# SSD stage of a hybrid encoder: masked product on VectorE, y gathered two chunks behind, decays times C made in place

## The chip, the cores and the metric

One core of a Trainium2 chip runs the whole program. The metric is the device time of one execution in microseconds (us), as the median of several. Engines: PE multiplies matrices, DVE is VectorE, ACT is ScalarE, POOL is GpSimd, SP is SyncE, which here issues DMAs.

## The reference, cut to what matters

Two layers on 1024 tokens of width 1024 in f32: dilated attention, then a bidirectional Mamba-2 SSD. The change concerns the second. For one direction, with 32 heads in 8 groups of 4, a state of 128 and chunks of 128 tokens:

```python
xbc = silu(depthwise_conv5(h @ w_in) + conv_b)
xdt = x * dt
acs = cumsum(dt * a)                           # within a chunk
decay = exp(where(lower, acs[l] - acs[s], -inf))
cb = einsum('bclgn,bcsgn->bcgls', C, B)
y_diag = einsum('bcgrls,bcsgrp->bclgrp', cb * decay, xdt)
states = einsum('bclgn,bclgrp->bcgrpn', B, xdt * exp(acs[-1] - acs))
prev = scan(states, exp(acs[-1]))              # state before each chunk
y_off = einsum('bclgn,cbgrpn->bclgrp', C, prev) * exp(acs)
```

The two directions and a skip term x d are added, the sum is multiplied by silu(z), normalised and projected back.

## The kernel before

**What runs beside what.** Layer 1 goes through the 8 groups. `group_dense(g)` makes the projection of group g: six tiles (x0, x1, B, C, z0, z1) of 128 channels x 1024 tokens, each in eight steps of six matmuls (L352 to L354; the f32 weights are split into a high part on ACT, L253, and a low part on DVE, L254). The first four tiles go through the convolution: ACT takes the middle tap out of PSUM (L1298), and four pairs of operations on DVE (L1306) add the other taps, straight from the accumulators. `ssd_items(g)` lists the SSD work of group g with weights, and `weave` puts it, in proportion to the weights, between the steps of the end of group g and the beginning of group g+1; for the last group it is woven into the output projection (`out1`: L976 to L978, with its y preparation L1485, L1502, L1507, L1508). What is emitted in this order is the order of every engine's queue.

**Accumulators.** Two of four PSUM banks hold a tile. Its four tap pairs are emitted in the tile that follows, behind steps 0, 1, 3 and 5, and the tile after that writes the same banks.

**The chunks of a group.** Behind the transposes (`A1`, L1364) and states (`A2`, L1376, L1377) come the chunks c from 7 down to 0, with four pieces:

- `B0(c)`: a DMA of 512 KB on SP (L1391) loads the decays, spread over all partitions, into `acs`, a pool of two buffers.
- `B1(c)`: ACT makes `ea`, the exponential of `acs` (L1401), DVE makes the four exponents E (L1404), PE the product of C and B (L1407), DVE masks it into cb (L1410), ACT takes the exponential of E (L1412) and writes four copies W of cb times dt (L1414). Then the load for c-2 is issued.
- `M(c)`: DVE multiplies ea by C in place (L1423), adds the other direction's cb times dt to W (L1428), and E times W, the masked product, is made on POOL, or on DVE in the last group and in chunk 0 (L1430).
- `B2(c)`: PE gathers y (L1441; 24 matmuls, 16 in chunks 7 and 0) from the states with ea and from x with the product; DVE adds the skip term (L1445, a pair of operations), POOL multiplies by silu(z) (L1449, two operations), and the last chunk sends the group's y to DRAM (L1454).

Before, `B2(c+1)` stands between `B1(c)` and `M(c)`. `dirs(c)` leaves out the direction that has no state yet, so the decays of chunks 7 and 0 have half the width.

Of the kernel before, what the change touches and what calls it, by code (L numbers as in the profile page):

```python
# [17 lines left out]
P = 128  # L18
# [55 lines left out]
class Trunk:  # L74
# [1272 lines left out]
    def ssd_items(self, g):  # L1347
# [7 lines left out]
        def ck(c):  # L1355
            return slice(P * c, P * c + P)
# [30 lines left out]
                    nc.vector.tensor_add(s, p, w)  # L1387

        def B0(c):
            a = live["a", c] = self.u("acs", [P, 2, 4, P], F32, 2)  # L1390
            nc.sync.dma_start(a, self.acsd[c, :, hs][None].to_broadcast([P, 2, 4, P]))  # L1391

        def dirs(c):
# [1 line left out]
            return [d for d, k in ((0, c > 0), (1, c < C - 1)) if k]  # L1395

        def B1(c):
            a = live.pop(("a", c))
            ea = live["ea", c] = self.u("ea", [P, 2, 4, P], F32, 2)
            ds = slice(dirs(c)[0], dirs(c)[-1] + 1)  # L1400
            nc.scalar.activation(ea[:, ds], a[:, ds], AF.Exp)  # L1401
            E, W = live["G", c] = [self.u("G", [P, 4, P], F32, 5) for _ in range(2)]
            for h in range(4):
                nc.vector.scalar_tensor_tensor(E[:, h], a[:, 0, h], self.delta[:, c, 4 * g + h:4 * g + h + 1], a[:, 1, h],  # L1404
                                               op0=OP.add, op1=OP.min)
            p = self.bank("a0", [P, P], 2)
            nc.tensor.matmul(p, st["B"][:, ck(c)], st["C"][:, ck(c)], start=True, stop=True)  # L1407
            cb = live["cb", c] = self.u("cb", [P, 2, P])
            tri = self.cst[:, CST["upper"][0]:CST["lower"][1]].rearrange("p (d l) -> p d l", d=2)
            nc.vector.tensor_mul(cb, p[:, None].to_broadcast([P, 2, P]), tri)  # L1410
            for h in range(4):
                nc.scalar.activation(E[:, h], E[:, h], AF.Exp, bias=self.nacb[:, c, 4 * g + h:4 * g + h + 1])  # L1412
            for h in range(4):
                nc.scalar.activation(W[:, h], cb[:, 0], AF.Copy, scale=self.dt[:, c, 4 * g + h:4 * g + h + 1])  # L1414
            if c == 0 and g < 7:
                nc.scalar.preload_act_table_set(SILU)
            if c > 1:
                B0(c - 2)

        def M(c):  # L1420
            ds = dirs(c)
            ea = live["ea", c][:, ds[0]:ds[-1] + 1].rearrange("p d h l -> p (d h) l")
            nc.vector.tensor_mul(ea, ea, st["C"][:, None, ck(c)].to_broadcast([P, 4 * len(ds), P]))  # L1423
            cb = live.pop(("cb", c))
            E, W = live["G", c]
            for h in range(4):
                hh = 32 + 4 * g + h
                nc.vector.scalar_tensor_tensor(W[:, h], cb[:, 1], self.dt[:, c, hh:hh + 1], W[:, h],  # L1428
                                               op0=OP.mult, op1=OP.add)
            (nc.vector if g == 7 or c == 0 else nc.gpsimd).tensor_mul(E, E, W)  # L1430

        def B2(c):

            y = self.bank("a3" if c % 2 else "a2", [P, 2, P])
            G, _ = live.pop(("G", c))
            ea = live.pop(("ea", c))
            for r in range(2):
                mms = [(SS[6 - c if d else c - 1][:, d], ea[:, d]) for d in dirs(c)] + [(xt[c], G)]
                for k, (w, m) in enumerate(mms):
# [17 lines left out]
        for j in range(C // 2):  # L1457
            items += [(200, lambda c=c: A1(c)) for c in (j, C - 1 - j)]
            if j:
                items.append((900, lambda j=j: A2(j - 1)))  # L1460
        items.append((1, lambda: (B0(C - 1), B0(C - 2))))
        items += [(900, lambda j=j: A2(j)) for j in range(C // 2 - 1, C)]
        if g == 7:
            items.append((1500, lambda: None))
        for c in range(C - 1, -1, -1):
            items.append((900, lambda c=c: B1(c)))
            if c < C - 1:
                items.append((500, lambda c=c: B2(c + 1)))
            items.append((1150, lambda c=c: M(c)))
        items += [(800, lambda: None), (500, lambda: B2(0))]  # L1470
        return items

    def out1(self, tail):
# [269 lines left out]
```

## Time and profile before

| | us |
|---|---|
| median of 3 runs (lowest, highest) | 1907.08 (1903.09, 1907.57) |
| the profiled execution | 1906.58 |
| its span in the profile | 1904.7 |

| engine | busy us | share of the span |
|---|---|---|
| PE | 1792.7 | 94% |
| DVE | 1404.3 | 74% |
| ACT | 957.8 | 50% |
| POOL | 392.7 | 21% |

The granted clock of PE was 0.98 of full speed over the span. A share is a mean over stages with different limits. A row of a timeline below gives start, duration, engine, line and operation, result and operands with their shapes, how many instructions are grouped (x4), and in brackets the idle time before it with what ended it. Group 2 of the SSD stage, which lies at 1207 to 1301 us, stands for the six groups 1 to 6, which have one pattern.

### The profile page before, as it was taken

To read this page: it belongs to the slowest core of one execution; us is meant where nothing else is said; L and a number is where in the kernel's file an instruction comes from. 1 tells how busy PE (TensorE), PEld (TensorE's weight loads), DVE (VectorE), ACT (ScalarE), POOL (GpSimd) and SP (SyncE) were. 2 spreads that over 40 slices of the span, in tenths; PEclk is the share of its full clock that TensorE was granted. 3 is DMA by queue.
4 is the path that set the end of the run, shared out by engine and by line. 5 is a ranking of instruction groups with operands and counts; after the bars stand their busy time and mean duration, and the time that the engine had idled before them with its cause. 6 is when DMAs were issued, how large, how long until landed. Compare 5 with 4: busy or idle time off the path is not lost.

```text
span 1904.7 us, 28678 instructions
## 1 busy us (share of the span) xinstructions
PE 1792.7 (94%) x10050; PEld 1450.5 (76%) x10050; DVE 1404.3 (74%) x3171; ACT 957.8 (50%) x2089; POOL 392.7 (21%) x541
## 2 busy tenths in 40 slices
PE   5899999999999999999989999999999999888997
PEld 3678788777788887779767777777777777666787
DVE  7867568667664665566767888888888888888875
ACT  5454445444454555444434655555555656555632
POOL 4611122112211311000101211212121212323310
PEclk7899999999999999999989999999999999999999
DMA  6242234222311321355113333333333333344643
GB/s 255 86 130 81 81 107 134 84 87 83 105 53 54 80 60 49 93 185 175 56 49 80 104 85 94 84 94 84 94 84 94 86 92 90 110 123 123 204 152 103
DMA packets 99735, 193.67 MB, mean 102 GB/s; under 512 B 15624, under 2 KB 23048, under 8 KB 99592
## 3 DMA queue, kind: packets, MB, share of 16 engines
q1 hardware_dynamic: 86600, 167.32, 28.9%
q0 software_dynamic: 12288, 23.86, 4.6%
q8 instruction: 80, 1.31, 0.3%
q10 hardware_dynamic: 704, 0.66, 0.1%
q14 instruction: 63, 0.52, 0.1%
HBM read 169.00 MB, written 16.48 MB: 97 GB/s over the span
## 4 chain that ended last, share of the span: by engine, by line
PE 26%; DVE 21%; ACT 6%; issue 3%; DMA 2%; POOL 0%; DVEq 0%; SPq 0%; ACTq 0%; POOLq 0%
DVE big L1306 5%; PE acc L352 4%; DVE G L1404 4%; PE acc L354 4%; PE acc L353 4%; DVE G L1428 3%; DVE ea L1423 3%; PE a L1377 3%; DVE wlo L254 2%; PE a L978 2%; PE a L976 2%; PE a L977 2%; PE acc L978 1%; PE acc L977 1%; PE acc L976 1%
## 5 line engine op out<-in xcount | busy, mean ns | idle before, releaser
L352 PE MATMUL acc<-big,whi 128*128 128x512 f32 (+1 forms) x1520 | 637.7, 420 | 24.0 <-ACT big L275 12.5
L353 PE MATMUL acc<-big,whi 128*128 128x512 f32 (+1 forms) x1520 | 596.9, 393 | 3.2 <-DVE big L276 3.1
L354 PE MATMUL acc<-big,wlo 128*128 128x512 f32 (+1 forms) x1520 | 597.1, 393 | 0.3 <-DVE wlo L254 0.3
L352 PEld LDWEIGHTS acc<-big,whi 128*128 128x128 f32 x1520 | 288.5, 190 | 88.3 <-issue 28.4
L354 PEld LDWEIGHTS acc<-big,wlo 128*128 128x128 f32 x1520 | 288.0, 189 | 65.1 <-DVE wlo L254 1.2
L353 PEld LDWEIGHTS acc<-big,whi 128*128 128x128 f32 x1520 | 289.5, 190 | 51.7 <-DVE big L276 6.5
L254 DVE TENSOR_TENSOR wlo<-wraw,whi 128x512 fp32r<-128x512 f32 (+1 forms) x298 | 214.4, 724 | 132.7 <-ACT whi L253 129.3
L253 ACT CAST whi<-wraw 128x512 fp32r<-128x512 f32 (+1 forms) x302 | 182.1, 611 | 84.5 <-PE a L977 27.4
L671 ACT ACTIVATE sm<-sm,nb 128x256 f32<-128x256 f32 (+1 forms) x192 | 89.3, 466 | 198.4 <-DVE nb L669 195.9
L1306 DVE SCALAR_TENSOR_TENSOR big<-acc,cv,big 128x512 f32<-128x512 f32 (+1 forms) x248 | 173.0, 740 | 2.2 <-ACT big L1298 2.2
L1412 ACT ACTIVATE G<-G,nacb 128x128 f32<-128x128 f32 x256 | 84.3, 391 | 154.9 <-DVE G L1404 154.1
L1430 POOL TENSOR_TENSOR G<-G,G 128x512 f32<-128x512 f32 x49 | 68.8, 1405 | 392.5 <-DVE G L1428 327.7
L682 DVE COPY pt<-a 128x512 f32<-128x512 f32 (+1 forms) x96 | 57.6, 600 | 76.5 <-PE a L680 76.5
L666 DVE CUSTOM_DVE_ANT_0 sm<-a,cst 128x256 f32<-128x256 f32 (+1 forms) x192 | 65.0, 376 | 64.3 <-PE a L661 64.0
L568 POOL DMA_DIRECT2D rt<-kT x92 | 50.5, 563 | 248.9 <-ACT kT L508 150.5
L1404 DVE SCALAR_TENSOR_TENSOR G<-acs,delta 128x128 f32<-128x128 f32 x256 | 99.3, 448 | 0.0
L976 PE MATMUL a<-big,whi 128*128 128x256 f32 (+1 forms) x304 | 99.3, 327 | 0.0
L978 PE MATMUL a<-big,wlo 128*128 128x256 f32 (+1 forms) x304 | 98.1, 323 | 0.9 <-DVE wlo L254 0.9
L977 PE MATMUL a<-big,whi 128*128 128x256 f32 (+1 forms) x304 | 97.9, 322 | 0.0
L1449 POOL TENSOR_TENSOR big<-big,yt 128x128 f32<-128x128 f32 x128 | 63.3, 515 | 159.5 <-DVE yt L1445 159.5
L976 PE MATMUL acc<-big,whi 128*128 128x512 f32 x224 | 91.1, 407 | 1.2 <-ACT big L253 1.2
L977 PE MATMUL acc<-big,whi 128*128 128x512 f32 x224 | 88.9, 397 | 2.4 <-DVE big L254 2.4
(255 smaller groups left out, 3198.5 us busy)
## 6 DMA issues: line engine op xcount, KB each, us to landing
wraw<-in_win SPq DMA_DIRECT2D x186, 256.0 KB
acs<-acsd SPq DMA_DIRECT2D x64, 512.0 KB
wraw<-in_wout SPq DMA_DIRECT2D x112, 256.0 KB
big<-in_modw SPq DMA_DIRECT2D x48, 512.0 KB
yd<-big POOLq DMA_DIRECT2D x14, 512.0 KB, 4.9
big<-yd SPq DMA_DIRECT2D x28, 256.0 KB
vT<-mix POOLq DMA_DIRECT2D x20, 256.0 KB, 4.5
big<-in_xT SPq DMA_DIRECT2D x8, 512.0 KB
```

The source lines that it names most:

```text
L253: self.nc.scalar.copy(dst_hi, src)
L254: self.late.append((lambda: self.lo_engine.tensor_sub(dst_lo, src, dst_hi.bitcast(F32)), tile))
L352: mm(o, hi[:, cols], x_[:, t0:t0 + n], start=first, stop=False, **kw)
L353: mm(o, hi[:, cols], x_[:, H2 + t0:H2 + t0 + n], start=False, stop=False, **kw)
L354: mm(o, lo[:, cols], x_[:, t0:t0 + n], start=False, stop=last, **kw)
L671: nc.scalar.activation(sm[:, h, :W], sm[:, h, :W], AF.Exp, bias=nb[:, h:h + 1], scale=0.125, accum_out=stat[:, h, 1, i:i + 1])
L976: mm(o, hi[:, c], x[:, t:t + n], start=kt == 0 and (n == H2 or m % 2 == 0), stop=False, **kw)
L977: mm(o, hi[:, c], x[:, H2 + t:H2 + t + n], start=False, stop=False, **kw)
L978: mm(o, lo[:, c], x[:, t:t + n], start=False, stop=kt == nkt - 1, **kw)
L1306: nc.vector.scalar_tensor_tensor(y[:, lo:hi], a[:, lo + o:hi + o], w[:, cv, k:k + 1], y[:, lo:hi], op0=OP.mult, op1=OP.add)
L1404: nc.vector.scalar_tensor_tensor(E[:, h], a[:, 0, h], self.delta[:, c, 4 * g + h:4 * g + h + 1], a[:, 1, h], op0=OP.add, op1=OP.min)
L1412: nc.scalar.activation(E[:, h], E[:, h], AF.Exp, bias=self.nacb[:, c, 4 * g + h:4 * g + h + 1])
```

## The change

- The masked product runs on DVE in all groups and chunks, behind the W add and ahead of decays times C.
- `acs` gets four buffers, and the exponential and decays times C are made in place in them; the pool `ea` goes. ACT makes that exponential behind the W copies instead of first. E and W get pools of three and two in place of five shared buffers.
- `B2(c+2)` stands between `B1(c)` and `M(c)`; `B2(1)` and `B2(0)` come at the end.
- The load `B0(c-1)` is issued ahead of `M(c)`, one at a time, in place of that for c-2 at the end of `B1(c)`.

```diff
         def B0(c):
-            a = live["a", c] = self.u("acs", [P, 2, 4, P], F32, 2)
+            a = live["a", c] = self.u("acs", [P, 2, 4, P], F32, 4)
...
         def B1(c):
-            a = live.pop(("a", c))
-            ea = live["ea", c] = self.u("ea", [P, 2, 4, P], F32, 2)
-            ds = slice(dirs(c)[0], dirs(c)[-1] + 1)
-            nc.scalar.activation(ea[:, ds], a[:, ds], AF.Exp)
-            E, W = live["G", c] = [self.u("G", [P, 4, P], F32, 5) for _ in range(2)]
+            a = live["a", c]
+            E, W = live["G", c] = self.u("E", [P, 4, P], F32, 3), self.u("W", [P, 4, P], F32, 2)
...
+            ds = slice(dirs(c)[0], dirs(c)[-1] + 1)
+            nc.scalar.activation(a[:, ds], a[:, ds], AF.Exp)
             if c == 0 and g < 7:
                 nc.scalar.preload_act_table_set(SILU)
-            if c > 1:
-                B0(c - 2)
...
         def M(c):
-            ds = dirs(c)
-            ea = live["ea", c][:, ds[0]:ds[-1] + 1].rearrange("p d h l -> p (d h) l")
-            nc.vector.tensor_mul(ea, ea, st["C"][:, None, ck(c)].to_broadcast([P, 4 * len(ds), P]))
...
-            (nc.vector if g == 7 or c == 0 else nc.gpsimd).tensor_mul(E, E, W)
+            nc.vector.tensor_mul(E, E, W)
+            ds = dirs(c)
+            a = live["a", c][:, ds[0]:ds[-1] + 1].rearrange("p d h l -> p (d h) l")
+            nc.vector.tensor_mul(a, a, st["C"][:, None, ck(c)].to_broadcast([P, 4 * len(ds), P]))
...
-        items.append((1, lambda: (B0(C - 1), B0(C - 2))))
+        items.append((1, lambda: B0(C - 1)))
...
             items.append((900, lambda c=c: B1(c)))
-            if c < C - 1:
-                items.append((500, lambda c=c: B2(c + 1)))
+            if c < C - 2:
+                items.append((500, lambda c=c: B2(c + 2)))
+            if c:
+                items.append((1, lambda c=c: B0(c - 1)))
             items.append((1150, lambda c=c: M(c)))
-        items += [(800, lambda: None), (500, lambda: B2(0))]
+        items += [(500, lambda: B2(1)), (900, lambda: None), (500, lambda: B2(0))]
```

A line that keeps its code gets another number: E is L1404 before and L1401 after, CB 1407 and 1404, the cb mask 1410 and 1407, the W add 1428 and 1423, the product 1430 and 1425, decays times C 1423 and 1428, the gather 1441 and 1439, the y pair 1445 and 1443, the gating 1449 and 1447.

In the rows below a name ends in a number that the buffer got. DVE in a steady group, from E of chunk 4 to the split behind its fourth tap pair, before:

```order
L1404 SCALAR_TENSOR_TENSOR G_11573<-acs_11432,delta_8965 128x128 x4
L1410 TENSOR_TENSOR cb_11581<-a_2131_11579,cst_71 128x256
L1445 SCALAR_TENSOR_TENSOR yt_11617<-big_10549,sv_8791,a_2137_11604 128x128
L1445 SCALAR_TENSOR_TENSOR yt_11617<-big_10714,sv_8791,a_2137_11604 128x128
L1306 SCALAR_TENSOR_TENSOR big_11478<-acc_11346,cv_8789,big_11478 128x510
L1306 SCALAR_TENSOR_TENSOR big_11478<-acc_11347,cv_8789,big_11478 128x512
L254 TENSOR_TENSOR wlo_11594<-wraw_11379,whi_11593 128x512
L1423 TENSOR_TENSOR ea_11571<-ea_11571,big_11035 128x1024
L1428 SCALAR_TENSOR_TENSOR G_11574<-cb_11581,dt_8962,G_11574 128x128 x4
L1404 SCALAR_TENSOR_TENSOR G_11656<-acs_11509,delta_8965 128x128 x4
```

The same stretch on DVE after:

```order
L1401 SCALAR_TENSOR_TENSOR E_11524<-acs_11488,delta_8965 128x128 x4
L1407 TENSOR_TENSOR cb_11532<-a_2108_11530,cst_71 128x256
L1306 SCALAR_TENSOR_TENSOR big_11444<-acc_11328,cv_8789,big_11444 128x511
L1306 SCALAR_TENSOR_TENSOR big_11444<-acc_11329,cv_8789,big_11444 128x512
L1443 SCALAR_TENSOR_TENSOR yt_11564<-big_10523,sv_8791,a_2110_11551 128x128
L1443 SCALAR_TENSOR_TENSOR yt_11564<-big_10682,sv_8791,a_2110_11551 128x128
L1423 SCALAR_TENSOR_TENSOR W_11525<-cb_11532,dt_8962,W_11525 128x128 x4
L1425 TENSOR_TENSOR E_11524<-E_11524,W_11525 128x512
L1428 TENSOR_TENSOR acs_11488<-acs_11488,big_11007 128x1024
L1306 SCALAR_TENSOR_TENSOR big_11444<-acc_11328,cv_8789,big_11444 128x510
L1306 SCALAR_TENSOR_TENSOR big_11444<-acc_11329,cv_8789,big_11444 128x512
L254 TENSOR_TENSOR wlo_11572<-wraw_11358,whi_11571 128x512
```

The third tap pair (128x511) moved behind E, the product joined, and W add, product and decays times C of this chunk moved ahead of the fourth tap pair (128x510).

PE in the same group, around the CB matmul of chunk 5 (128x128 into a PSUM tile `a`), before:

```order
L352 MATMUL acc_11482<-big_8684,whi_11376 128x512
L353 MATMUL acc_11482<-big_8684,whi_11376 128x512
L354 MATMUL acc_11482<-big_8684,wlo_11377 128x512
L1407 MATMUL a_2120_11497<-big_11035,big_10879 128x128
L352 MATMUL acc_11481<-big_8035,whi_11376 128x512
L353 MATMUL acc_11481<-big_8035,whi_11376 128x512
L354 MATMUL acc_11481<-big_8035,wlo_11377 128x512
L352 MATMUL acc_11482<-big_8689,whi_11376 128x512
L353 MATMUL acc_11482<-big_8689,whi_11376 128x512
L354 MATMUL acc_11482<-big_8689,wlo_11377 128x512
L1441 MATMUL a_2126_11524<-ea_11412,SS_11321 64x128 x2
```

And after:

```order
L352 MATMUL acc_11329<-big_8736,whi_11285 128x512
L353 MATMUL acc_11329<-big_8736,whi_11285 128x512
L354 MATMUL acc_11329<-big_8736,wlo_11286 128x512
L1404 MATMUL a_2096_11453<-big_11007,big_10845 128x128
L352 MATMUL acc_11466<-big_8031,whi_11355 128x512
L353 MATMUL acc_11466<-big_8031,whi_11355 128x512
L354 MATMUL acc_11466<-big_8031,wlo_11356 128x512
L352 MATMUL acc_11467<-big_8684,whi_11355 128x512
L353 MATMUL acc_11467<-big_8684,whi_11355 128x512
L354 MATMUL acc_11467<-big_8684,wlo_11356 128x512
L1439 MATMUL a_2100_11474<-acs_11219,SS_11324 64x128 x2
```

Before, a step of the new tile stands ahead of this CB (its `big_8684` is the first operand of the tile's first step), and the gather that follows is that of chunk 6; after, the tile begins behind the CB, with the banks `acc_11466` and `acc_11467`, and the gather is the first of the group, that of chunk 7.

SP in the last group, from the load of the decays for chunk 6 on, before:

```order
L1391 DMA acs_15881<-acsd 128x2x512
L1485 DMA big_15902<-yd 128x512
L325 DMA wraw_15913<-in_wout 128x512
L1485 DMA big_15932<-yd 128x512
L1485 DMA big_15974<-yd 128x512
L325 DMA wraw_15990<-in_wout 128x512
```

And after, from the load for chunk 7 to that for chunk 6:

```order
L1391 DMA acs_15823<-acsd 128x2x512
L1485 DMA big_15844<-yd 128x512
L325 DMA wraw_15855<-in_wout 128x512
L1485 DMA big_15874<-yd 128x512
L1485 DMA big_15916<-yd 128x512
L325 DMA wraw_15932<-in_wout 128x512
L1485 DMA big_15965<-yd 128x512
L325 DMA wraw_15973<-in_wout 128x512
L325 DMA wraw_15978<-in_wout 128x512
L1391 DMA acs_16008<-acsd 128x2x512
```

The load for chunk 6 moved behind the reads of y and four weight loads.

## Rows read from the trace of the kernel before

**Rows 1.** Windows; columns: stretch, us, busy by engine, PE clock, DMA share, GB/s.
```profile
1207.00:1301.00 94.00, 90.81 (x535) 72.17 (x534) 78.48 (x168) 52.43 (x120) 17.92 (x26) 1.00 0.31 90
1212.00:1228.00 16.00, 15.48 (x104) 12.27 (x103) 15.98 (x35) 9.99 (x24) 4.55 (x6) 1.00 0.41 99
...
1694.00:1747.00 53.00, 42.27 (x262) 32.76 (x261) 52.13 (x100) 35.71 (x83) 20.32 (x21) 0.90 0.44 135
```

**Rows 2.** Waits of PE, 1010 to 1750; columns: total us, times, longest us.
```profile
PE a L1441 <- POOL G L1430: 15.8, 29, 1.7
PE a L1441 <- DVE G L1430: 7.2, 6, 2.6
...
PE a L1441 <- DVE ea L1423: 4.2, 3, 3.1
```

**Rows 3.** Timeline of DVE, group 2.
```profile
1203.79 0.69 DVE L254 TENSOR_TENSOR wlo<-wraw,whi 128x512 fp32r<-128x512 f32 x1 [3.42 <-ACT whi L253]
...
1213.18 2.16 DVE L1404 SCALAR_TENSOR_TENSOR G<-acs,delta 128x128 f32<-128x128 f32 x4
...
1215.61 1.39 DVE L1306 SCALAR_TENSOR_TENSOR big<-acc,cv,big 128x512 f32<-128x512 f32 x2
1216.92 0.59 DVE L1445 SCALAR_TENSOR_TENSOR yt<-big,sv,a 128x128 f32<-128x128 f32 x2
...
1219.36 1.21 DVE L1423 TENSOR_TENSOR ea<-ea,big 128x1024 f32<-128x1024 f32 x1
...
1222.86 1.14 DVE L1404 SCALAR_TENSOR_TENSOR G<-acs,delta 128x128 f32<-128x128 f32 x4
...
1224.88 1.40 DVE L1306 SCALAR_TENSOR_TENSOR big<-acc,cv,big 128x510 f32<-128x510 f32 x2
...
1229.06 2.16 DVE L1404 SCALAR_TENSOR_TENSOR G<-acs,delta 128x128 f32<-128x128 f32 x4
...
1260.60 1.14 DVE L1428 SCALAR_TENSOR_TENSOR G<-cb,dt,G 128x128 f32<-128x128 f32 x4
1261.77 0.69 DVE L1430 TENSOR_TENSOR G<-G,G 128x512 f32<-128x512 f32 x1
1262.38 0.74 DVE L1306 SCALAR_TENSOR_TENSOR big<-acc,cv,big 128x512 f32<-128x512 f32 x1
```

**Rows 4.** Timeline of PE, group 2.
```profile
1211.50 0.39 PE L352 MATMUL acc<-big,whi 128*128 128x512 f32 x1
...
1212.86 0.38 PE L1407 MATMUL a<-big,big 128*128 128x128 f32 x2
1213.00 0.48 PE L352 MATMUL acc<-big,whi 128*128 128x512 f32 x1
...
1220.38 0.48 PE L352 MATMUL acc<-big,whi 128*128 128x512 f32 x1
...
1223.12 0.44 PE L1441 MATMUL a<-G,xt 128*64 128x128 f32 x4 [0.52 <-POOL G L1430]
...
1227.00 0.39 PE L352 MATMUL acc<-big,whi 128*128 128x512 f32 x1
...
1262.61 0.44 PE L1441 MATMUL a<-G,xt 128*64 128x128 f32 x4 [0.65 <-ACT big L1310]
```

**Rows 5.** Timeline of ACT, group 2.
```profile
1208.57 1.27 ACT L1414 ACTIVATE G<-cb,dt 128x128 f32<-128x128 f32 x4
```

**Rows 6.** Timeline of DVE, group 0.
```profile
1033.91 1.33 DVE L1428 SCALAR_TENSOR_TENSOR G<-cb,dt,G 128x128 f32<-128x128 f32 x4
```

**Rows 7.** The page's part 5, one group; columns: busy us, mean ns, idle ahead.
```profile
L1449 POOL TENSOR_TENSOR big<-big,yt 128x128 f32<-128x128 f32 x128 | 63.3, 515 | 159.5 <-DVE yt L1445 159.5
```

**Rows 8.** The page's part 6, one issue; columns: size, us to landing.
```profile
yd<-big POOLq DMA_DIRECT2D x14, 512.0 KB, 4.9
```

**Rows 9.** Timeline of SP, last group.
```profile
1672.01 12.32 SPq L325 DMA_DIRECT2D wraw<-in_wout  x2
```

**Rows 10.** Timeline of DVE, last group.
```profile
1693.90 1.35 DVE L1508 SCALAR_TENSOR_TENSOR big<-big,sv,big 128x512 fp32r<-128x512 f32 x1 [2.85 <-ACT big L1507]
```

More of the change, by code (lines that the diff above doesn't have):

```diff
@@ L1435, in B2 @@
             G, _ = live.pop(("G", c))
-            ea = live.pop(("ea", c))
+            ea = live.pop(("a", c))
             for r in range(2):
```

## The prediction

> **What bounds the kernel now.** The page's first part gives PE 94% of the span, so the question for a change to the SSD stage is where PE does not run there, and what it waits for. The SSD work of group g is woven into the projection of group g+1; group 2 lasts 94.00 us, with PE busy 90.81 and DVE 78.48 [rows 1]. These means hide two phases. In the first half of the chunks (1211 to 1258) DVE is busy 15.98 of 16 us [rows 1]; behind it, where the states are made, it has about 15 us to spare. PE's waits over the groups are nearly all on the y matmuls, for the masked product or the decays: 15.8, 7.2 and 4.2 us [rows 2], over 7 groups some 4 us each. The reader is to see that PE and DVE are both near their limit in the same stretch: PE is short of work because the product comes late, and the product comes late because DVE, which feeds POOL, is full.
>
> There is a second coupling that costs nothing now. A projection tile writes two of four accumulator banks; the tile two later takes them again, once the four tap pairs (L1306) have read them. The fourth tap pair of the tile begins on DVE at 1224.88, so its first half is over at 1225.6 [rows 3], and the next tile's first matmul comes at 1227.00 [rows 4]: 1.4 us of slack.
>
> **Prices.** On DVE one instruction starts 0.07 to 0.09 us before the one ahead of it has ended, in every row of [rows 3] where the successor does not need the result (1261.77 lasts 0.69, the next begins 0.61 later). In this counting: weight split 0.60, tap pair 1.31, y pair 0.52, decays times C 1.13 (half width, chunks 7 and 0, an estimate of 0.61), the four E operations 1.07, E and cb mask together 1.40 (1213.18 to 1215.61 less the 1.02 named below), W add up to the product 1.17, because the product waits for its end (1260.60 to 1261.77), product 0.61 (1261.77 to 1262.38) [rows 3]. On PE a step of six matmuls is 1.36 (1211.50 to 1212.86), the CB matmul 0.14, and a chunk without a wait 7.38 (1213.00 to 1220.38) [rows 4]: four steps and CB leave 1.80 for one gather of y.
>
> **The product on DVE.** 49 products leave POOL (15 are on DVE already). Each costs DVE 0.61 and the 0.12 by which 1.17 exceeds the 1.05 of a W add that nobody waits for: 0.73. Against that, the POOL product runs beside the E operations of the next chunk in one chunk of two and stretches them to 2.16 from 1.14 [rows 3], 1.02 that goes away. A tile holds two chunks: 2 x 0.73 - 1.02 = +0.44 per tile on a DVE that is full.
>
> **The gather two chunks behind.** It is emitted after its product by more than a chunk (7.4 us) instead of 2 to 4 us, so PE's waits of [rows 2] go. What is late next? The first gather moves behind the CB of chunk 5, so PE comes to each tile sooner and the SSD work stands about 0.8 step earlier against the taps. PE would start the second tile at 1227.00 less a 16-matmul gather (two thirds of 1.80, 1.2), less 0.6 because the two gathers in the tile are now 16 and 24 matmuls, less its stall of 0.52 [rows 4]: 1224.7, or 1224.0 with the stall of the first gather gone as well. DVE decides whether the banks are free by then. I follow it from the split at 1203.79 [rows 3], behind which the row order of after puts: W add of chunk 7 at 1204.39, product 1205.56, decays times C 1206.17, E and cb of chunk 6 from 1206.78 to 1208.2. The W add then waits for ScalarE's W copies, which end near 1209.8 [rows 5], so the product starts at 1210.0; decays times C, split, E of chunk 5 at 1212.4. Chunk 5 holds E and cb 1.40, y 0.52, tap 1.31, W add 1.17, product 0.61, decays 1.13, tap 1.31, split 0.60: 8.05, to 1220.4. In chunk 4 the whole of M now stands ahead of the fourth tap pair: 1.40 + 1.31 + 0.52 + 1.17 + 0.61 + 1.13 = 6.14, to 1226.6; its first half ends at 1227.3. PE, ready at 1224.0 to 1224.7, waits some 3 us for it. So the wait for the product is replaced by one for a bank, and the tile starts no earlier than the 1227.00 of now.
>
> **POOL's gating beside the W add.** The gating multiplications (L1449) stay on POOL. In chunks 4 and 2 they will run beside the W add, where before taps stood, which read PSUM. The one place of before where this happens shows the W add at 1.33 instead of 1.14 [rows 3, 6]: 0.2 for each of the two, 0.42 per chunk, which I take since the row is of the same pair of operations; the ends are 0 and the full length of both, 2 x 0.515 [rows 7]. It moves the second tile's start to 1227.75, +0.75.
>
> The Trainium skill, page "SBUF — State Buffer", section "SBUF: two separate sides", says that the port pair shared by VectorE and GpSimd is an exclusive lock: of a VectorE operation with two SBUF inputs and a GpSimd operation, the one that starts first holds it for its whole length, the other fully blocks. The 1.02 that E loses agrees with a lock for most of the product; the 0.2 of the W add is less than the lock would make of it. By the rule the sum would be that of the last rival below.
>
> **Second tile.** DVE's pair of chunks takes 15.88 now (1213.18 to 1229.06 [rows 3]). Less 1.02, plus 1.46 for the products, plus 0.42 for POOL, plus 0.60 in which the tile's first y pair stands on DVE before its gather is done (the gather ends one step and 1.80 after the tile's first matmul, 3.1 us, while DVE reaches the y pair some 2.5 us after the tap that freed the bank): 17.34, against the 15.88 of now. +0.75 + 1.5 = +2.25 at the third tile. The 0.60 is the loosest of these; its ends are 0 and 1.
>
> **Third tile, and the end of the chunks.** Here M of chunk 0 stands behind the last taps, DVE needs about 14.0, and PE bounds: 2 x 7.38 = 14.76 against 15.9 now, so the fourth tile is at +1.1. Then one gather that stood earlier (chunk 1) comes behind: +1.80, less that tile's stall at chunk 0 of 0.65 [rows 4] and some 0.2 around it. +0.92. A steady group: **+2.0 us**, from +0.6 (no POOL loss, no y wait) to +3.2 (a full lock).
>
> **What costs nothing.** The decays are read four chunks deep, and the 512 KB load is issued one chunk further ahead of the E that needs it; the only transfer of this size whose landing the profile shows took 4.9 us [rows 8]. The tightest lead, for chunk 1, I estimate at one chunk, 7.38, so the work of that chunk hides it with some 2 us to spare. If that cover went, E would stall DVE by what is missing. Exp moved behind the W copies is ScalarE time that was there before; ScalarE is busy 52.43 of 94.00 [rows 1], and decays times C comes last in M, over 2 us after.
>
> **The last group** (1637 to 1747) runs beside the output projection. DVE is busy 52.13 of 53.00 in its chunks, and the product is on DVE there already [rows 1]. Here the load for chunk 6 moves on SP's queue behind a weight load that waits for its slot; SP stood 12.32 us in these loads until 1684.3 [rows 9], and E of chunk 6 is next on DVE. With 4.9 to landing DVE stalls about 5; 2.85 of it was idle a little later anyway [rows 10], and other work can give some: +1.5, bounds -3 and +4. The gathers were seldom late there, so little is won.
>
> **Sum.** Six steady groups 6 x 2.0 = 12.0; the first, whose weave starts otherwise, +1 (-1 to +2); the last +1.5: +14.5. The profiled execution took 1906.58, half a microsecond under the median of 1907.08, and the sum made against it gives 1921.1.
>
> **Rivals.** A, faster: the banks never gate. It decides whether the fourth tap pair is through by 1224.7 in the second tile; then all of PE's waits of [rows 2] go, 27.2 us, and the smaller ones of the same matmuls with them, some 31 in all: 1875. For it: PE names only these waits, and DVE has 15 us to spare per group. Against it: that spare time lies behind the chunks, and in them DVE has 0.02 of 16 us [rows 1]; the slack is 1.4 us now and 2.9 us of M move ahead of the tap. Where DVE's chain would be shorter by 3 us, for instance because ScalarE's copies come sooner in the earlier order, the gain begins to show.
>
> B, no difference: POOL's gating does not slow the W add, and the y pair finds its gather done. Second tile +0.33, third +0.8, fourth -0.3, end +0.6: 6 x 0.6 + 1 + 1.5 = +6 at most, near 1911. For it: only one row shows the 1.33, and both costs hang on a few tenths of order in time. Against: the order of after puts the y pair straight ahead of the W add in both chunks.
>
> C, slower still: the gating blocks DVE whole, 1.03 instead of 0.42 in chunks 4 and 2, +1.2 a group, 1929. For: E beside the POOL product lost nearly that much in proportion. Against: 1.33 is measured beside the same operation.
>
> **Chances.** The forecast 0.60, A 0.12, B 0.16, C 0.12. About 0.3%, 5.7 us, is what a measurement of this kernel can tell from no change: faster is below 1901.4, slower above 1912.8. A is faster, B is same, the forecast and C are slower: 0.12, 0.16, 0.72. The range leaves most of A out: from 1903, with a part of B's lower side and the last group's -3, to 1931, with C.
>
> **What would show it.** Right: PE's waits for the product gone, and in their place waits of the projection's first matmul for L1306, of 2 to 4 us in the second tile and less in the third; E always 1.14; the W add at 1.33 beside the gating in chunks 4 and 2; a group period of 96; in the last group DVE waiting for the decays' load before E of chunk 6. Wrong, if PE waits for L1306 nowhere and the period falls to 90 (A), if DVE waits at E in the steady groups (the load is not covered), or if the y pair shows no wait (B).

## The result: 1937.4 us, and the profile of the changed kernel

The changed kernel takes 1937.38 us (1934.30 to 1941.06) beside 1906.34 for the kernel before: a ratio of 1.0166 (95% interval 1.0144 to 1.0189). 1.7% slower was found, 0.8% forecast; the time lies above the range. The profiled execution, the longest of four, took 1941.06, 34.5 more than that of before.

The page of the changed kernel, busy time and the slices of PE's granted clock:

```profile
PE 1806.3 (93%) x10050; PEld 1464.9 (76%) x10050; DVE 1417.7 (73%) x3220; ACT 951.4 (49%) x2089; POOL 326.4 (17%) x492
...
PEclk7899999999999999999899999999999999999999
```

PE does the same 10050 matmuls and is busy 13.6 us longer with them; the mean granted clock is 0.969 instead of 0.98 (the digits of the slices, whole tenths, are too coarse to show it). That is the first sign of what the prediction left out.

Waits of PE, 1010 to 1790 us, after (line waited for: total us, times, longest), which answer to [rows 2]:

```profile
PE acc L352 <- DVE big L1306: 39.3, 14, 3.5
PE acc L977 <- DVE big L1508: 10.5, 5, 4.1
...
PE a L1439 <- DVE yt L1443: 2.0, 1, 2.0
```

Waits of DVE over the same stretch, after:

```profile
DVE yt L1443 <- PE a L1439: 22.2, 19, 3.3
...
DVE E L1401 <- DMA acs<-acsd: 8.4, 1, 8.4
```

The waits for the product are gone, as meant and as forecast. In their place PE waits twice in each of the seven groups for the taps to leave a bank, and the y pair on DVE waits for its gather: both had been forecast, the second as 0.6 us a group. The timeline of PE, group 2 after, around the second tile of the chunks:

```profile
1232.18 0.38 PE L1404 MATMUL a<-big,big 128*128 128x128 f32 x2
1236.02 0.76 PE L352 MATMUL acc<-big,whi 128*128 128x512 f32 x1 [3.46 <-DVE big L1306]
1236.58 0.63 PE L353 MATMUL acc<-big,whi 128*128 128x512 f32 x1
...
1238.85 1.12 PE L1439 MATMUL a<-acs,SS 128*64 128x128 f32 x8
...
1241.61 0.73 PE L352 MATMUL acc<-big,whi 128*128 128x512 f32 x1
```

Windows of the same stretch (stretch, us, busy by engine, PE clock, DMA share, GB/s), after:

```profile
1235.30:1242.10 6.80, 6.08 (x31) 4.74 (x32) 3.52 (x10) 3.90 (x10) 0.00 (x0) 0.50 0.12 42
1242.10:1249.00 6.90, 6.90 (x48) 5.58 (x49) 6.87 (x16) 0.07 (x1) 0.89 (x2) 1.00 0.00 0
```

After 3.46 us without work PE's clock is at 0.50 of full speed, 1.2 GHz: a 128x512 matmul is 0.63 long instead of 0.39. The gather, which PE has to make before DVE can go on, ends late, and DVE pays. Its timeline there, after, against [rows 3]:

```profile
1228.64 1.13 DVE L1401 SCALAR_TENSOR_TENSOR E<-acs,delta 128x128 f32<-128x128 f32 x4
...
1231.86 1.50 DVE L1423 SCALAR_TENSOR_TENSOR W<-cb,dt,W 128x128 f32<-128x128 f32 x4
...
1235.13 1.40 DVE L1306 SCALAR_TENSOR_TENSOR big<-acc,cv,big 128x510 f32<-128x510 f32 x2
...
1241.80 0.61 DVE L1443 SCALAR_TENSOR_TENSOR yt<-big,sv,a 128x128 f32<-128x128 f32 x2 [3.28 <-PE a L1439]
...
1248.46 1.13 DVE L1401 SCALAR_TENSOR_TENSOR E<-acs,delta 128x128 f32<-128x128 f32 x4
```

The pair of chunks 4 and 3, E to E, takes 19.82 where 17.34 was forecast; 3.28 of it is the y pair standing still. The windows show it too: DVE is busy 3.52 of 6.80 in the first, where the clock is at 0.50, and 6.87 of 6.90 in the second, where it is at 1.00. Here the fall costs because slow matmuls of PE delay the engine that PE had been waiting for.

How long a group takes, from the first transpose (L1364) of one to that of the next, in the profiled executions, and whether the clock fell (a stretch at 0.50 between 1010 and 1640):

| kernel | first group | groups 1 to 6, mean (lowest, highest) | last group to the end | falls in 1010 to 1640 |
|---|---|---|---|---|
| before | 87.8 | 93.99 (93.89, 94.02) | 263.7 | 0 |
| changed | 91.9 | 97.80 (97.26, 98.94) | 270.8 | 9 |

### The profile page after: what moved, and what is told of

Same layout as the page of the kernel before. It is cut to its first block, busy times and chain, and to the rows that moved or that the text cites. A ratio compares the mean times of both kernels' runs of the same rounds, so it can differ in the third digit from the quotient of the medians.

```text
span 1939.3 us, 28460 instructions
## 1 busy us (share of the span) xinstructions
PE 1806.3 (93%) x10050; PEld 1464.9 (76%) x10050; DVE 1417.7 (73%) x3220; ACT 951.4 (49%) x2089; POOL 326.4 (17%) x492
## 4 chain that ended last, share of the span: by engine, by line
PE 33%; DVE 16%; ACT 4%; DMA 3%; issue 3%; SPq 0%; DVEq 0%; POOL 0%; ACTq 0%; POOLq 0%
PE acc L352 6%; PE acc L354 5%; PE acc L353 5%; DVE big L1306 3%; PE a L1439 3%; DVE acs L1428 3%; PE a L1377 2%; DVE W L1423 2%; DMA acs<-acsd 2%; DVE wlo L254 2%; PE a L976 2%; PE a L977 2%; PE a L978 2%; PE acc L978 1%; PE acc L977 1%
## 5 line engine op out<-in xcount | busy, mean ns | idle before, releaser
L1409 ACT ACTIVATE E<-E,nacb 128x128 f32<-128x128 f32 x256 | 82.0, 391 | 211.8 <-DVE E L1401 172.5
L1306 DVE SCALAR_TENSOR_TENSOR big<-acc,cv,big 128x512 f32<-128x512 f32 (+1 forms) x248 | 172.9, 743 | 0.0
L978 PE MATMUL acc<-big,wlo 128*128 128x512 f32 x224 | 90.5, 404 | 5.2 <-DVE wlo L254 4.9
L1439 PE MATMUL a<-acs,SS 128*64 128x128 f32 x896 | 78.8, 293 | 5.6 <-issue 2.5
```

Of the source, the lines that this page charges most:

```text
L978: mm(o, lo[:, c], x[:, t:t + n], start=False, stop=kt == nkt - 1, **kw)
L1306: nc.vector.scalar_tensor_tensor(y[:, lo:hi], a[:, lo + o:hi + o], w[:, cv, k:k + 1], y[:, lo:hi], op0=OP.mult, op1=OP.add)
L1439: nc.tensor.matmul(y[64 * i:64 * i + 64, r], w[:, 2 * r + i], m[:, 2 * r + i], start=k == 0, stop=k == len(mms) - 1)
```

## The experiments

Ratios are to the kernel before on the same chip, with 95% intervals. In what was expected, "the third and fourth projection tile (B and C)" are the tiles that the prediction calls the second and third of the chunks.

### The clock held up by matmuls that nobody reads

```diff
+            if kt == 0 and warm:
+                p = self.bank("a0", [P, H2], 2)
+                for k in range(warm):
+                    self.nc.tensor.matmul(p, self.whl[b][0][:, :P], x[0][:, :H2], start=k == 0, stop=k == warm - 1)
             self.mm3(accs, self.whl[b + i], slice(c, c + P), x, kt == 0, kt == KT - 1)
...
-            tiles.append(self.dense(self.wb["in1"] + 2 * (6 * g + m), e, banks) if g or m > 1 else None)
+            tiles.append(self.dense(self.wb["in1"] + 2 * (6 * g + m), e, banks, (0, 0, 15, 9, 0, 0)[m] if g else 0) if g or m > 1 else None)
```

> The changed kernel with matmuls that nobody reads ahead of the first matmul of the third and fourth projection tile (B: 15 of 128x512, 3.4 us; C: 9, 2.0 us), so that PE is busy where it waits for the banks. Theory 1 (the wait for the taps makes the granted clock fall, and PE at 1.2 GHz then keeps VectorE waiting for y): the clock stays at 1.00 from 1010 to 1640, the waits of the y pair in the second tile of the chunks fall from 3.3 us to about 0.7, a group takes 95.5 to 96.5 instead of 97.3 to 98.9, the whole 1919 to 1925. Theory 2 (VectorE's longer chain alone sets the time, the clock is a by-product): within 4 us of the 1937 of the changed kernel.

Measured: 1924.46, ratio 1.0092 (1.0075 to 1.0109). Groups 1 to 6 take 95.77 (95.72 to 95.83). Timeline of PE, then of DVE, with the extra matmuls (line numbers behind the edit are four higher):

```profile
1228.75 3.69 PE L376 MATMUL a<-big,whi 128*128 128x512 f32 x15
1232.38 0.50 PE L352 MATMUL acc<-big,whi 128*128 128x512 f32 x1
...
1249.59 0.50 PE L352 MATMUL acc<-big,whi 128*128 128x512 f32 x1
```

```profile
1225.08 1.13 DVE L1405 SCALAR_TENSOR_TENSOR E<-acs,delta 128x128 f32<-128x128 f32 x4
...
1231.58 1.40 DVE L1310 SCALAR_TENSOR_TENSOR big<-acc,cv,big 128x510 f32<-128x510 f32 x2
...
1235.62 0.61 DVE L1447 SCALAR_TENSOR_TENSOR yt<-big,sv,a 128x128 f32<-128x128 f32 x2 [0.65 <-PE a L1443]
...
1242.29 1.14 DVE L1405 SCALAR_TENSOR_TENSOR E<-acs,delta 128x128 f32<-128x128 f32 x4
```

And its window over group 2:

```profile
1200.00:1296.00 96.00, 95.61 (x558) 76.80 (x558) 80.06 (x175) 51.33 (x119) 8.21 (x18) 1.00 0.32 88
```

More work on PE makes the kernel 13 us faster. The clock is 1.00, the y pair waits 0.65 (0.60 in the prediction), and the pair of chunks takes 17.21 (17.34). The scatter between the groups is gone too. The extra matmuls only fill the wait: the tile starts 0.80 us after the fourth tap pair with them (1231.58 to 1232.38) and 0.89 without (1235.13 to 1236.02). So 2.03 us a group, 12.2 in six, is the clock, and theory 1 holds. The profiled executions lie 18.9 us apart; 4.8 of that is in the last group, where no extra matmul runs and DVE waits 5.6 for the decays instead of 8.4, and 1.9 stands ahead of the first group.

### The product back on GpSimd; the product alone on VectorE

```diff
-            nc.vector.tensor_mul(E, E, W)
+            (nc.vector if g == 7 or c == 0 else nc.gpsimd).tensor_mul(E, E, W)
```

> The changed kernel with the masked product back on GpSimd where it was before. Theory 1 (VectorE's chain ahead of the fourth tap pair is too long): four products of 0.61 less and the E operations stretched again by 1.0, so the wait for the bank falls from 3.5 to about 2, the clock seldom falls, a group takes 94 to 95.5, the whole 1908 to 1918. Rival (the product on VectorE is the whole loss, the later gather a gain): the whole under 1900. Rival (the later gather is the whole loss): above 1930.

Measured: 1917.33, ratio 1.0051 (1.0036 to 1.0066). PE's waits for a bank are still 25.8 us, in group 2 one of 2.98 and one of 0.78. The clock falls in all steady groups but one: that one takes 93.92, the others 95.33 to 95.47. Theory 1's time was right; its wait of about 2 and its "seldom falls" were not.

The other way round, in the kernel before:

```diff
-            (nc.vector if g == 7 or c == 0 else nc.gpsimd).tensor_mul(E, E, W)
+            nc.vector.tensor_mul(E, E, W)
```

> The kernel before with the masked product on VectorE everywhere, nothing else. Theory 1: 0.44 us per tile more on a full VectorE, the order of taps and M as before, so no wait for a bank over 1 us and no fall of the clock; 1 to 2 us a group, the whole 1912 to 1920. Rival (the product on VectorE is the whole loss): 1930 or more.

Measured: 1920.33, ratio 1.0066 (1.0051 to 1.0081), 0.3 above what was expected; the clock does fall, which had not been expected. Windows over its groups 2 and 3, without and with a fall, and the row of PE's timeline that stands ahead of the fall in group 1:

```profile
1175.80:1270.70 94.90, 90.93 (x533) 72.15 (x532) 77.50 (x173) 51.52 (x119) 6.96 (x16) 1.00 0.33 88
1270.70:1367.20 96.50, 92.52 (x533) 73.30 (x532) 80.11 (x177) 51.52 (x119) 9.28 (x21) 0.98 0.33 88
```

```profile
1171.95 0.44 PE L1441 MATMUL a<-G,xt 128*64 128x128 f32 x4 [1.34 <-ACT big L1310]
```

Three of its steady groups (2, 4, 5) take 94.92 to 94.95, three (1, 3, 6) 96.33 to 96.49; the trace has three falls in them, at 1172.4, 1363.5 and 1650.3, one near the end of each of groups 1, 3 and 6. Without a fall the product alone costs 0.95 us a group, with one 1.5 more. In the groups without a fall the same 1.34 stands at the same place.

### The same work, with M behind the last taps again

```diff
+        items.append((1000, lambda: None))
         for c in range(C - 1, -1, -1):
```

> The changed kernel with an empty item of weight 1000 ahead of chunk 7, which puts the masked product and decays times C of chunks 4 and 2 behind the fourth tap pair again, as in the kernel before; all work is the same. Theory 1 (the M that stands ahead of the last tap pair holds the bank): the wait for the bank at the second and third tile under 1.5 us, the clock stays up in the groups, the W add is never beside the gating, a group takes 93.5 to 95.5, the whole 1908 to 1920. Rival (the amount of VectorE work sets it, whatever the order): 1930 or more.

Measured: 1908.65, ratio 1.0008 (0.9999 to 1.0018): all that the change cost is back, though VectorE does the same operations. Timeline of PE, group 2:

```profile
1229.54 0.47 PE L352 MATMUL acc<-big,whi 128*128 128x512 f32 x1 [0.76 <-DVE big L1306]
...
1246.82 0.47 PE L352 MATMUL acc<-big,whi 128*128 128x512 f32 x1 [1.97 <-DVE big L1306]
```

The second tile's wait went from 3.46 to 0.76; the third's stayed at 1.97, more than the 1.5 expected, and the clock still falls in four of the groups 1 to 6. But five of the six groups take 94.42 to 94.46, with a fall (three of them) or without (two); only group 1, with a fall, takes more, 94.83. Groups 1 to 6 take 94.51, the last 261.5. Theory 1's time holds, its claim on the clock only in part: a fall is not costly by itself.

### The taps earlier

```diff
-                    late.setdefault((2, 3 + i) if g == m == 0 else (3 if g == 0 and m == 1 else m + 1, (0, 1, 3, 5)[i]),
+                    late.setdefault((2, 3 + i) if g == m == 0 else (3 if g == 0 and m == 1 else m + 1, (0, 1, 2, 3)[i]),
```

> The changed kernel with the four tap pairs emitted behind steps 0, 1, 2 and 3 of the next tile instead of 0, 1, 3 and 5, so that the last of them stands ahead of M of chunks 4 and 2. Theory (what stands ahead of the last tap pair holds the bank): bank waits under 1.5 us, no fall of the clock in groups 1 to 6, a group 93.5 to 95.5, the whole 1908 to 1920. Rival (the amount of VectorE work sets the pace): 1930 or more.

Measured: 1933.01, ratio 1.0138 (1.0119 to 1.0156): the rival. Waits of PE, and the row of its timeline in group 2:

```profile
PE a L1439 <- DVE yt L1443: 23.4, 7, 3.5
PE acc L352 <- DVE big L1306: 9.5, 12, 1.4
```

```profile
1272.53 0.44 PE L1439 MATMUL a<-acs,SS 128*64 128x128 f32 x4 [3.47 <-DVE yt L1443]
```

The bank waits fell from 39.3 to 9.5 as expected, and the time did not: DVE is still behind, and the lag shows at the end of the group, where the last gather waits 3.47 us for the y pair that reads its PSUM buffer. The clock falls there instead. The bank is thus not the cause by itself: it is one of the places where a full DVE lets PE stand. Beside the kernel with the empty item, which does the same work, the difference that shows is the length of the single wait and the fall that follows it; no run changes that length alone.

### The load for chunk 6, and GpSimd's gating

```diff
-        items.append((1, lambda: B0(C - 1)))
+        items.append((1, lambda: (B0(C - 1), B0(C - 2))))
...
-            if c:
-                items.append((1, lambda c=c: B0(c - 1)))
+            if c > 1:
+                items.append((1, lambda c=c: B0(c - 2)))
```

> The changed kernel with the loads of the decays issued two chunks ahead, those of chunks 7 and 6 together, as in the kernel before, but from the place of the changed kernel. Theory (the load for chunk 6 behind the weight loads is what the last group loses): VectorE's wait of 8.4 us for it goes, the last group takes 264 to 267 instead of 270.8, the whole 1930 to 1935, the seven groups as they are. Rival (VectorE is behind there anyway and catches up): within 2 us of the changed kernel.

Measured: 1932.53, ratio 1.0137 (1.0119 to 1.0155), 4.9 us under the changed kernel by the medians. The last group takes 264.1 instead of 270.8. What is gone is this, in the timelines of SP and DVE of the changed kernel:

```profile
1699.84 11.73 SPq L325 DMA_DIRECT2D wraw<-in_wout  x2
1711.63 0.43 SPq L1391 DMA_DIRECT2D acs<-acsd  x1
```

```profile
1720.16 1.14 DVE L1401 SCALAR_TENSOR_TENSOR E<-acs,delta 128x128 f32<-128x128 f32 x4 [8.37 <-DMA acs<-acsd]
```

The load stands 11.73 us behind the weight loads, is issued at 1711.6, and DVE starts 8.5 us later.

The steady groups of this kernel take 97.80 on the mean, as in the changed kernel, and they hold a test of the clock's price that needs no extra matmuls. PE's row at the second tile of group 3, and windows of groups 3 and 4:

```profile
1332.40 0.47 PE L352 MATMUL acc<-big,whi 128*128 128x512 f32 x1 [3.47 <-DVE big L1306]
```

```profile
1275.50:1371.36 95.86, 89.85 (x533) 72.45 (x532) 79.80 (x175) 51.37 (x119) 8.23 (x19) 1.00 0.31 89
1371.36:1470.03 98.67, 92.89 (x533) 74.83 (x532) 79.79 (x175) 51.43 (x119) 8.20 (x19) 0.97 0.32 86
```

Group 3 has the full wait of 3.47 but no fall, and takes 95.86, the 95.77 of the kernel with the extra matmuls. Groups 1, 5 and 6, with one stretch at 0.50, take 97.37 to 97.51; groups 2 and 4, with two, 99.93 and 98.67. The wait at the second tile is 3.47 or 3.48 in all six, so what the time above 95.86 goes with is the fall and not the wait ahead of it.

The gating was taken out of the kernel with the extra matmuls, where the clock does not fall in groups 1 to 6; y of groups 0 to 6 is then not multiplied by silu(z):

```diff
-                nc.gpsimd.tensor_mul(z, z, t[:, r])
+                if g == 7:
+                    nc.gpsimd.tensor_mul(z, z, t[:, r])
```

> The kernel with the extra matmuls, and without the gating multiplications on GpSimd in groups 0 to 6 (y isn't multiplied by silu(z) there). Theory (GpSimd beside the W add costs VectorE 0.37 in chunks 4 and 2): every W add 1.13 instead of 1.50, 0.75 a group, 95.1 instead of 95.8, the whole 1918 to 1920. Rival (GpSimd blocks more than the W add shows): 1915 or less. Rival (it costs nothing on the path): within 2 us of the 1924.5 with the gating.

Measured: 1920.06, ratio 1.0075 (1.0055 to 1.0095); the interval overlaps that of the kernel with the gating, so the groups must tell: 95.19 in each of the six, 0.58 less, and 89.7 instead of 92.0 in the first, which also loses its one fall of the clock. The W add of chunk 4 in this kernel, and the gating that stood beside it in the changed kernel:

```profile
1226.58 1.13 DVE L1427 SCALAR_TENSOR_TENSOR W<-cb,dt,W 128x128 f32<-128x128 f32 x4
```

```profile
1231.75 0.92 POOL L1447 TENSOR_TENSOR big<-big,yt 128x128 f32<-128x128 f32 x2 [8.42 <-DVE yt L1443]
```

1.50 became 1.13 in chunks 4 and 2, 0.74 a group, of which 0.58 reaches the end.

### What is left of the change without these costs

Product on GpSimd, the loads two chunks ahead, and 12 and 2 extra matmuls.

```diff
-            nc.vector.tensor_mul(E, E, W)
+            (nc.vector if g == 7 or c == 0 else nc.gpsimd).tensor_mul(E, E, W)
...
-        items.append((1, lambda: B0(C - 1)))
+        items.append((1, lambda: (B0(C - 1), B0(C - 2))))
...
+                for k in range(warm):
+                    self.nc.tensor.matmul(p, self.whl[b][0][:, :P], x[0][:, :H2], start=k == 0, stop=k == warm - 1)
...
```

> The changed kernel with the product on GpSimd, the loads two chunks ahead, and extra matmuls ahead of the third and fourth tile (12 and 2): what is left of the change is the later gather, the decays made in place, and the order. Theory (fall of the clock, product, and the load for chunk 6 are the whole loss; the later gather alone gains and costs nothing): a group 93.5 to 94.2, no fall of the clock in groups 1 to 6, the whole 1902 to 1910, the kernel before within 0.3%. Rival (the later gather costs as such, by its y pair and the gather at the end): a group 95 or more, the whole 1912 to 1920.

Measured: 1907.21, ratio 0.9999 (0.9990 to 1.0008), groups 1 to 6 at 93.78 (93.76 to 93.80), no fall of the clock in them. With the clock held up, the gather two chunks behind and the decays in place cost nothing and gain 0.2 us a group. Between this kernel and the one with the extra matmuls alone stand 1.99 us a group: the product on VectorE and what it leads to. The two differ in the loads and in the number of extra matmuls too, but the groups without a fall and without extra matmuls give nearly the same: 93.92 with the product on GpSimd, 95.86 with it on VectorE.

### Towards a faster kernel: combinations, and more time for the chunks

Taps early, product on GpSimd, loads two chunks ahead:

```diff
-                    late.setdefault((2, 3 + i) if g == m == 0 else (3 if g == 0 and m == 1 else m + 1, (0, 1, 3, 5)[i]),
+                    late.setdefault((2, 3 + i) if g == m == 0 else (3 if g == 0 and m == 1 else m + 1, (0, 1, 2, 3)[i]),
...
-            nc.vector.tensor_mul(E, E, W)
+            (nc.vector if g == 7 or c == 0 else nc.gpsimd).tensor_mul(E, E, W)
...
```

> The changed kernel with the taps at steps 0 to 3, the product on GpSimd as before, and the loads two chunks ahead: the gather two chunks behind with none of the costs found so far. Theory: VectorE has 0.44 us less per tile than with the product, PE waits neither for the product nor long for a bank; a group 92.5 to 94, the whole 1893 to 1906, at or below the kernel before. Rival (the later gather costs as such, by its y pair and the gather of chunk 1 at the end): 1908 to 1915.

Measured: 1926.61, ratio 1.0102 (1.0087 to 1.0118), slower than both cases that had been thought of. As with the early taps alone, PE waits at the end of each group for the y pair (23.6 us, 7 times, up to 3.7), and the clock falls there (groups 1 to 6 take 95.91 to 96.64). The waits moved, they did not go.

VectorE is full beside the chunks and has some 15 us free beside the states [rows 1]. The weights of the weave say how many of PE's steps each gets. In the kernel before:

```diff
-                items.append((900, lambda j=j: A2(j - 1)))
+                items.append((600, lambda j=j: A2(j - 1)))
...
-        items += [(900, lambda j=j: A2(j)) for j in range(C // 2 - 1, C)]
+        items += [(600, lambda j=j: A2(j)) for j in range(C // 2 - 1, C)]
```

> The kernel before with the weight of the state items (A2) at 600 instead of 900, nothing else: the states get fewer of PE's steps and the chunks more, 4.4 steps a chunk instead of 4.1. Theory (VectorE is full only beside the chunks and has 15 us free beside the states): PE's waits for the product shrink, a group takes 90.5 to 93, the whole 1880 to 1900. Rival (the states' own chain is then late, PE waits there instead): 1904 to 1915.

Measured: **1895.72**, ratio 0.9950 (0.9935 to 0.9965): faster than both kernels. Groups 1 to 6 take 93.01. Windows of two stretches beside the chunks of one group, and PE's waits, in this kernel:

```profile
1210.00:1226.00 16.00, 16.00 (x107) 12.86 (x106) 14.66 (x34) 6.97 (x19) 5.17 (x7) 1.00 0.25 72
1226.00:1242.00 16.00, 13.97 (x96) 10.88 (x94) 14.81 (x32) 9.10 (x21) 4.69 (x5) 1.00 0.37 102
```

```profile
PE acc L352 <- DVE big L1306: 9.0, 6, 1.5
...
PE a L1441 <- POOL G L1430: 5.0, 7, 1.9
```

DVE has over a microsecond free in 16 where it had 0.02 [rows 1], and the waits for GpSimd's product fell from 15.8 to 5.0. A bank wait of 1.5 per group came in their place, and the clock does not fall in groups 1 to 6. The listed waits do not hold the whole gain of 0.98 a group: PE's idle time in a group falls by 0.2 only, while its busy time, which can hide short pauses, goes from 90.82 to 90.04 for the same 534 matmuls.

The same weights in the changed kernel with the loads two chunks ahead:

```diff
-                items.append((900, lambda j=j: A2(j - 1)))
+                items.append((600, lambda j=j: A2(j - 1)))
...
```

> The changed kernel with the loads of the decays two chunks ahead and the weight of the state items at 600. Theory (the pace of VectorE beside the chunks is what makes the bank waits, and these the falls of the clock): with 7% more PE time per chunk the bank waits stay under 1.5 us, the clock stays up in groups 1 to 6, a group takes 91 to 94, the whole 1885 to 1908, more than 25 us under the 1932.5 that the earlier loads alone give. Rival (the work ahead of the last tap pair decides, whatever the pace): 1920 or more.

Measured: 1930.41, ratio 1.0136 (1.0119 to 1.0152): the expectation failed, groups 2 to 6 take 98.6 to 98.95. Timelines of PE and ACT:

```profile
1263.76 0.76 PE L352 MATMUL acc<-big,whi 128*128 128x512 f32 x1 [4.71 <-ACT big L1298]
```

```profile
1257.38 1.28 ACT L1409 ACTIVATE E<-E,nacb 128x128 f32<-128x128 f32 x4 [6.14 <-DVE E L1401]
...
1262.18 1.44 ACT L1298 ACTIVATE big<-acc,cv 128x512 f32<-128x512 f32 x2
```

With the new weights the evacuation of a tile (L1298) stands on ScalarE behind the exponential of the last chunk, which waits 6.14 us for DVE's E; a wait of 4.71 for the bank follows, and the clock falls in each of the groups 1 to 6. A long single wait with a fall behind it stands again, at a new place.

> As the run before, with the product on GpSimd. Theory: 0.4 us less on VectorE per tile; where the pace is no longer VectorE's the product's place no longer matters, so within 5 us of the run before; where it is, 5 to 10 us less. Rival (GpSimd's product costs VectorE by contention more than it takes off): 5 us or more above it.

The same kernel with the product on GpSimd:

```diff
-            nc.vector.tensor_mul(E, E, W)
+            (nc.vector if g == 7 or c == 0 else nc.gpsimd).tensor_mul(E, E, W)
```

Measured: 1914.07, ratio 1.0044 (1.0029 to 1.0059), 16 us less than with the product on VectorE, where at most 10 had been expected. PE's waits for L1298 halve, from 28.2 to 14.7 us: 2.9 instead of 4.7 at the longest.

## Why the prediction was wrong

The direction and the mechanism were right: the wait for the product became a wait for a bank, and the sum of it was positive. The size was off by 20 us in the profiled execution, 14.5 forecast and 34.5 found. Step by step:

- **The wait for the bank.** Forecast some 3 us at the second tile, found 3.46. PE waits for L1306 there in every group.
- **Its price was taken as its own length, and this is the step that failed.** PE comes out of it at 0.50 of its clock, and the prediction had no term for that. The experiment with the extra matmuls gives the term: 97.80 less 95.77, 2.03 us a group, 12.2 in six. A group that keeps the wait but has no fall (95.86, with the loads two chunks ahead) says the same. With the falls gone a steady group costs 1.78 more than before, beside the +2.0 of the sum, and the terms hold one by one: counted from the first transpose of group 2 (1170.90 before, 1175.56 with the extra matmuls), the second tile starts 0.72 later than before (1227.00 [rows 4] and 1232.38; forecast 0.75), the third 2.08 later (1242.85, below, and 1249.59; forecast 2.25). The trace of before had the warning in its last group, where the window of 1694 to 1747 shows the clock at 0.90 [rows 1]. The Trainium skill, page "TensorE: Matmul & The Clock Gate", section "Part 1: The HAM clock gate (the "warmup" mystery)", says that a block watches how busy PE has been and passes half the clock pulses where it has been idle; by that rule a long single wait is likelier to bring a fall than several short ones of the same sum. The trace agrees as far as it goes, the sums being unlike: before, 15.8 us of waits for GpSimd's product in 29 pieces of at most 1.7 [rows 2] brought no fall in 1010 to 1640; after, 37.0 us in 13 waits for the taps there, and one of 2.0 for the y pair, brought nine.

  PE before, at the third tile of group 2:

```profile
1242.85 0.39 PE L352 MATMUL acc<-big,whi 128*128 128x512 f32 x1
```

- **The y pair.** Forecast 0.60 a group, "its ends are 0 and 1"; found 0.65 at full clock and 3.28 behind a fall. The pair of chunks was forecast at 17.34 and took 17.21 and 19.82. The first number was right, the bounds were wrong, because they were made for one PE clock.
- **GpSimd beside the W add.** The sum took 0.2 for each of the two gatings, 0.42 a chunk; found 0.37 (1.50 for 1.13). The 1.33 named as the sign is what one gating costs in [rows 6]. With both taken away the groups are 0.58 shorter. Rival C, both gatings blocking DVE for their whole length, would have made that 0.92 here; 0.37 was measured, so its mechanism did not occur, though its time was nearer. The full lock that the Trainium skill states for such a pair (page "SBUF — State Buffer", section "SBUF: two separate sides") is thus not what this row shows.
- **The product on VectorE.** Forecast +0.44 a tile. Alone, in the kernel before, it costs 0.95 a group where the clock stays up, about two tiles' worth; in the changed kernel, with the taps behind it and GpSimd beside the W add, 1.99. The sum holds the two together: 1.99 less the 0.2 that the rest of the change gains is the 1.78 beside its +2.0.
- **The last group.** Forecast +1.5 with an upper bound of +4, found +7.1. The place was right; the size was not. 4.9 was taken from another queue's transfer, and DVE started 8.5 us after the issue, its own wait 8.37. Loads two chunks ahead bring 6.7 of it back.
- **The first group.** +1 was written down without a working; 4.1 was found. The product alone, in the kernel before, brings 3.1 there, with one fall of the clock in it; with the product back on GpSimd the first group takes 88.8, 1.0 more than before.
- **The loads in the steady groups.** Covered, as forecast: DVE waits for the decays once in the program, in the last group.
- **A reading of [rows 2].** "Over 7 groups some 4 us each" is not so: that window reaches into the last group, where nearly all of the 7.2 and the 4.2 lie (up to 1640 they are 0.8 and 0.3). Group 2 waited 2.0 us for the product, so rival A had less to win than its 31 us. The sum does not use this figure.

The miss of 20 is thus 12.2 from the clock, 5.6 from the last group and 3.1 from the first, less 1.3 (6 x 0.22) in the steady groups: 19.6.

What stays open: why the same wait brings a fall in one group and none in the next (below), why falls cost nothing in most groups of the kernel with the empty item, and why the early taps end a group with a wait of 3.47 us where the empty item, with the same work, ends it (group 2) with one of 1.47.

## What to carry to other kernels

Price a wait of PE by its length and by what follows it: where a change makes a single wait longer (here 3.46 us where no wait of a steady group had been over 0.7), look at the granted clock and at who waits for PE next, since a slow PE hands the loss back to the engine that it was waiting for. Where two engines are both full in a stretch, the order chooses the place of the wait, and its price has to be measured at each place: the empty item brought back the whole loss, the earlier taps almost none of it. Only more time for that stretch, from one in which the second engine is idle, made the kernel before faster (0.5%); the same weights gained 2 us in the changed kernel (1930.4 beside 1932.5), where a new wait came up. And look at each moved load on its queue for what waits in front of it, with a landing time from the same queue.

## What the runs showed of the hardware

- A fall of the clock is not certain for a given wait. In groups 1 to 6 of the changed kernel the clock fell in a wait of 3.46 or 3.47, or within 1.4 us behind it, in five of six cases, behind waits of 2.0 to 2.4 in two of six. In the kernel before with the product on VectorE it fell behind a wait of 1.34 that ended at 1171.95, and not behind one that ended at 1268.42. Groups of one kernel differ by 1.5 us with it (product on VectorE in the kernel before), by up to 4.1 with the loads two chunks ahead (95.86 without a fall, 99.93 with two).
- Matmuls that do nothing but fill a wait went with a kernel 13 us faster, 1937.4 to 1924.5, and no fall of the clock in groups 1 to 6.
- The four VectorE operations of a W add, with two SBUF inputs each, lost 0.37 together beside two GpSimd multiplications of 0.92 together (1.50 for 1.13); the four E operations beside GpSimd's masked product lost 1.02 (2.16 for 1.14 [rows 3]).
